# Hybrid attention block on one core: FFN gemms interleaved singly, wide matmuls of a product first, queries ahead of the retention transposes, a table load and a copy moved

## The chip, the core and the metric

The kernel runs on one core of a Trainium2 chip. The core has a matrix engine (TensorE, PE in the profile), a vector engine (VectorE, DVE), an activation engine (ScalarE, ACT), GpSimd (POOL) and SyncE (SP, which here issues most DMA transfers). Each engine takes its own instructions in order and waits on semaphores for the others. Operands lie in SBUF, matmuls write PSUM, which has eight banks of 128 partitions x 512 fp32 numbers. The metric is the device time of one execution in microseconds (us), as the median of several runs.

## The reference

One transformer block for 512 tokens of width 1024, all in fp32. Its core, cut:

```python
mod = einsum('bd,de->be', silu(c), w_ada) + b_ada        # shift1, scale1, gate1, shift2, ...
hmix = modulate(rmsnorm(x, g_norm1), shift1, scale1)
sb_q, sb_k, sb_v, r_q, r_k, r_v, r_g, br = split(einsum('bsd,de->bse', hmix, w_in))
o_sb = stick_breaking_attention(sb_q, sb_k, sb_v)         # 16 heads of 64
o_ret = retention(rotary(r_q), rotary(r_k) * 256 ** -0.5, r_v)   # 4 heads, qk 256, v 512
o_ret = silu(r_g) * head_rmsnorm(o_ret)
g_sb, g_ret = split(sigmoid(br + b_branch))
merged = g_sb * (o_sb @ w_proj_sb) + g_ret * (o_ret @ w_proj_ret)
x = x + gate1 * (merged @ w_out)
hffn = modulate(rmsnorm(x, g_norm2), shift2, scale2)
a, u = split(hffn @ w_ffn_in)                             # 2816 columns each
x = x + gate2 * ((silu(a) * u) @ w_ffn_out)
return rmsnorm(x, g_final)
```

## The kernel before

Everything is kept transposed: features on the partitions, the 512 tokens along the free dimension. The weights come packed in `wp` and stay fp32 in memory. A fp32 product is made of three matmuls in the faster type fp32r: each operand is split into a high and a low part (`split`, L206 on ACT for the high copy, L208 on DVE for the difference), and PE adds high x high, high x low and low x high (`mm3`, all recorded at L228). `gemm` runs this over the pieces `k` of the contraction: a gemm with eight pieces is 24 matmuls, one with four is 12. `weight` loads a raw weight over SP's queue and splits it into `whi` and `wlo`; `low` and `high` (L851, L847) do the same for sums of weights, and `low_dma` has the subtraction done by a DMA.

PSUM's eight banks belong to three pools: `ps` (4), `z` (3) and `av` (1). SBUF tiles come from pools too, with few buffers each (weights: raw 3, whi 4, wlo 4). A scheduler orders the instructions of each engine by when it expects their operands and by their order in the program; in blocks under `manual_schedule` the program's order is kept as written.

**The retention heads.** For each head the queries and keys (`ret_qk`) are two gemms of 24 matmuls each (two halves of 256 features, in two `ps` banks), followed by the rotary multiplications on DVE (from L674 on). The scores and outputs follow (`ret_scores`, `ret_out`), which leave the head's output in four banks (three of `z` and `av`). `ret_gate` finishes a head: four multiplications on DVE, each with the norm's factor and the gate's Silu (L758), then 16 transposes on PE of 128 x 128 blocks into the same pools' banks (L762), whose results are split on ACT and DVE into pairs `s` for the projection. The loop over `h` (L1045 on) does, for heads 0 to 2: the gate of head `h`, the queries and keys of head `h + 1`, and then `seven`, which holds the projection of head `h` (`ret_proj`) and the values and gates of head `h + 1`, computed as seven products of half-size blocks (a scheme of Strassen's kind: sums of blocks of weights and of activations, seven products for eight). Head 3's gate stands ahead of the attention's values (`seven("sv", ...)`), in the mode `first=True`: the first product runs ahead of the gate, and its copies (L991) are on ACT. Just ahead of it `sigmoid_tables` (L329) loads ACT's function table for what follows.

**The FFN.** The 2816 hidden features are 11 blocks `p` of 256. For each `p`, `a` and `u` come from seven products (p, 1) to (p, 7) of the same kind. For p from 2 (`WIDE`) on, a product is `wide_product`: it writes two banks, and for each bank it multiplies the high weight with high and low activations side by side (512 wide) four times, and the low weight with the high activations (256 wide, into the bank's second half) four times. `both_sums` and `both_added` (ACT copy, then DVE additions, L1304 and L1312) empty the two banks. Products 1, 6, 7 and 4 of a `p` share the two `ps` banks called `z`, products 5 and 3 two others, product 2 uses two of the `z` pool. `store_act` splits the result. The second gemm of the FFN (`out`, eight feature blocks, 12 matmuls each) takes the hidden features in chunks of up to two `p`, and its results are added to the residual (L1158).

The list `work` sets the order: the seven products of each `p` as (1, 5, 6, 2, 7, 3, 4), with out gemms of the chunk before in between, two after product 5 and two after product 4. Ahead of each item, the weights of the items up to `AHEAD` places later are loaded and split (`prepare_item`). The FFN's opening (L1480 to L1600) is a manual block: it computes the second norm by halves and runs the products of p = 0, some of p = 1 and the first two of p = 2 in a written order; `held_pe`, `held_act` and `held` are the instructions behind which the scheduler may place what follows.

Of the kernel before, what the change touches and what calls it, by code (L numbers as in the profile page):

```python
# [115 lines left out]
def kernel(  # L116
# [545 lines left out]

    def ret_qk(h, banks=None):
        res = []
        for key in ("rq", "rk"):
            if banks:
                p1, p2 = banks.pop(0), banks.pop(0)
            else:
                p1, p2 = ps(), ps()
                gemm(p1, weight((key, h, 0)), hs)  # L670
                gemm(p2, weight((key, h, 1)), hs)
            for c1, c2, op in ((cosT, sinT, ALU.subtract), (sinT, cosT, ALU.add)):
                m1, m2 = tmp(), tmp()
                nc.vector.tensor_mul(m1, p1, c1)  # L674
                nc.vector.tensor_mul(m2, p2, c2)
                nc.vector.tensor_tensor(m1, m1, m2, op=op)
                hl = pair("q")
                split(hl[:, 0, :], hl[:, 1, :], m1)
                res.append(hl)
        return res  # L680
# [364 lines left out]
    for h in range(3):  # L1045
        ys = ret_gate(h, *outs, sgs)
        qk = ret_qk(h + 1)
        st, outs = {}, []
# [3 lines left out]
        sgs = [rsgs[b] for b in range(4)]  # L1052
    act_table = sigmoid_tables()
    seven("sv", 3, lambda: ret_gate(3, *outs, sgs), sv_store, first=True)

# [186 lines left out]
    def prepare_item(it):  # L1242
        if it[0] == "out":
            ready[it] = out_weight(*it[1:])
            return
# [44 lines left out]
    def wide_product(p, n, banks, first, last):  # L1290
        hi, lo = (tiles(t) for t in ready.pop((p, n)))
        for i, o in enumerate(banks):
            c = slice(i * P, (i + 1) * P)
            for k in range(4):
                mm(o, hi[:, k, c], act7(SEVEN[n], k)[2], first and k == 0, False)
            for k in range(4):
                mm(o[:, 256:S], lo[:, k, c], act7(SEVEN[n], k)[0], False, last and k == 3)
# [109 lines left out]

    def run_out(c, i):
        for j, w in enumerate(ready.pop(("out", c, i))):
            o = psa() if j else psz()  # L1410
            gemm(o, w, ff_acts[c])
            residual(2 * i + j, o, 40)

    NP, NC, AHEAD = NF // 2, len(FF_CHUNKS), 5
    chunk_of = {p: c for c, (p0, n) in enumerate(FF_CHUNKS) for p in range(p0, p0 + n)}
# [4 lines left out]
    for c, (p0, n) in enumerate(FF_CHUNKS):  # L1422
        for p in range(p0, p0 + n):
            wide = p >= 2
            for n_, m in enumerate((1, 6, 5, 2, 7, 3, 4) if p == 1 == WIDE else (1, 5, 6, 2, 7, 3, 4) if wide else (1, 6, 5, 7, 2, 4, 3)):
                if (p, m) not in FIRST:
                    work.append((p, m))
                    if n_ in ((1, 6) if wide else (2, 5)) and len(outs) > (1 if c == NC - 1 else 0):
                        work.append(outs.pop(0))
        work += outs  # L1430
        outs = [("out", c, i) for i in range(4)]
    for m in (2, 1):
# [33 lines left out]
    with tc.manual_schedule(engines={nc.vector.engine, nc.scalar.engine, nc.tensor.engine}):  # L1466
# [114 lines left out]
        nc.vector.tensor_add(d1["s0"], d1["x2"], d1["p1"])  # L1581
        for d in (d0, d1):
            nc.scalar.activation(d["s0"], d["s0"], AF.Silu)
        d0["u3"] = tmp()
# [4 lines left out]
        k6 = high(t1[6], wtile("whi"))  # L1589
        nc.scalar.activation(d0["u3"], d0["u3"], AF.Silu)  # L1590
        d2 = part.setdefault(2, {})
        d2["x"] = ps()
        product(2, 1, d2["x"], True, False)
        d2["p1"] = tmp()
        held_act = nc.scalar.activation(d2["p1"], d2["x"], AF.Copy).ins
        ready[1, 6] = low(t1[6], k6, wtile("wlo"))
# [19 lines left out]
    for it in work:  # L1616
# [3 lines left out]
        with after_opening():  # L1620
            (run_out if it[0] == "out" else run_product)(*it[-2:])
    ln_exp_tables()
# [167 lines left out]
```

## Time and profile before

| | |
|---|---|
| median of 3 runs | 1121.58 us |
| lowest and highest | 1119.62 and 1122.04 us |
| the profiled execution | 1119.72 us |
| its span | 1118.0 us |
| mean granted TensorE clock | 0.997 |
| PE busy | 1101.4 us (99%) |
| DVE busy | 876.9 us (78%) |
| ACT busy | 562.4 us (50%) |
| POOL busy | 42.2 us (4%) |

The profile records one execution. A row of a timeline has the start of a group of like instructions in us from the span's start, the time from the first's start to the last's end, engine, source line, operation, the tiles written and read (buffer numbers left out), the shape, the count, and in brackets the idle time of the engine ahead of the group with the engine and line that ended it. Matmuls are pipelined, so the length in a row is longer than what a matmul adds: the distance from one start to the next tells the pace. The rows use the lines of the kernel before; a weight `whi` or `wlo` belongs to the gemm whose matmuls read it.

### The profile page before, as it was taken

How to read it: one execution, taken by the hardware profiler on the slowest of the kernel's cores; microseconds unless marked ns; L12 is line 12 of the kernel's file. 1: busy time of each engine (PE TensorE's matmuls, PEld its weight loads, DVE VectorE, ACT ScalarE, POOL GpSimd, SP SyncE). 2: the span in 40 equal slices, each digit the busy share in tenths (PEclk: the TensorE clock that was granted, in tenths of full speed). 3: DMA queues.
4: the chain of work that ended last, by engine and by line, in shares of the span. 5: the costliest groups of instructions: out<-in, count | busy, mean ns of one | idle time of the engine just before them, and what ended most of it. 6: DMA issues, size and time to landing. Idle time of an engine off the chain costs nothing.

```text
span 1118.0 us, 15104 instructions
## 1 busy us (share of the span) xinstructions
PE 1101.4 (99%) x5607; PEld 934.7 (84%) x5607; DVE 876.9 (78%) x1315; ACT 562.4 (50%) x926; POOL 42.2 (4%) x69
## 2 busy tenths in 40 slices
PE   8999999999999999999999999999999999999996
PEld 6888888888788788888888888899988888888886
DVE  7899756959977969387777866567999988888866
ACT  5445345444444645365565654357645544554443
POOL 0000000010020020000000000000000000000000
PEclk9999999999999999999999999999999999999998
DMA  9814432766785476876676459662444444444112
GB/s 360 301 57 152 145 118 79 224 133 207 244 168 179 160 163 214 241 208 184 171 200 173 141 182 311 207 170 58 132 133 132 132 132 123 123 132 128 62 38 77
DMA packets 60554, 181.42 MB, mean 162 GB/s; under 512 B 7488, under 2 KB 9536, under 8 KB 60480
## 3 DMA queue, kind: packets, MB, share of 16 engines
q1 hardware_dynamic: 54464, 166.30, 45.9%
q0 software_dynamic: 5472, 13.63, 7.7%
q8 instruction: 44, 0.72, 0.3%
q10 hardware_dynamic: 544, 0.52, 0.1%
q14 instruction: 30, 0.25, 0.1%
HBM read 148.97 MB, written 16.78 MB: 148 GB/s over the span
## 4 chain that ended last, share of the span: by engine, by line
PE 82%; DVE 11%; DMA 3%; ACT 2%; issue 1%; SPq 0%; DVEq 0%; ACTq 0%
PE ps L228 61%; PE z L228 12%; PE av L228 7%; DMA araw<-wada 3%; DVE araw L256 2%; DVE wlo L851 1%; PE ps L636 1%; DVE s L870 1%; DVE wlo L208 1%; DMA sraw<-wada 1%; DVE t L758 0%; ACT whi L847 0%; PE z L762 0%; DVE s L209 0%; DVE t L1033 0%
## 5 line engine op out<-in xcount | busy, mean ns | idle before, releaser
L228 PE MATMUL ps<-h,whi 128*128 128x512 f32 (+1 forms) x1026 | 294.9, 372 | 0.0
L228 PEld LDWEIGHTS ps<-h,whi 128*128 128x128 f32 x1026 | 185.3, 189 | 32.0 <-issue 0.5
L206 ACT ACTIVATE whi<-raw 128x1024 fp32r<-128x1024 f32 (+1 forms) x104 | 108.6, 1044 | 195.7 <-PE ps L228 154.8
L228 PE MATMUL ps<-h,wlo 128*128 128x512 f32 (+1 forms) x513 | 188.0, 370 | 0.0
L208 DVE TENSOR_TENSOR wlo<-raw,whi 128x1024 fp32r<-128x1024 f32 (+1 forms) x104 | 125.0, 1201 | 65.1 <-ACT whi L206 64.6
L228 PEld LDWEIGHTS ps<-h,wlo 128*128 128x128 f32 x513 | 96.7, 188 | 16.7
L228 PE MATMUL ps<-q,whi 128*128 128x512 f32 (+1 forms) x368 | 103.8, 388 | 0.0
L228 PE MATMUL ps<-s,whi 128*128 128x512 f32 x320 | 98.9, 390 | 0.5 <-DVE s L208 0.3
L851 DVE TENSOR_TENSOR wlo<-s,whi 128x1024 fp32r<-128x1024 f32 x46 | 56.1, 1222 | 42.3 <-ACT whi L847 42.3
L228 PEld LDWEIGHTS ps<-q,whi 128*128 128x128 f32 x368 | 65.2, 188 | 10.9
L847 ACT ACTIVATE whi<-s 128x1024 fp32r<-128x1024 f32 x47 | 49.6, 1057 | 45.6 <-PE ps L228 35.0
L228 PE MATMUL ps<-whi,h 128*128 128x512 f32 x222 | 71.7, 391 | 0.0
L228 PEld LDWEIGHTS ps<-s,whi 128*128 128x128 f32 x320 | 60.1, 188 | 13.5 <-DVE s L208 0.6
L228 PE MATMUL ps<-q,wlo 128*128 128x256 f32 (+1 forms) x328 | 63.4, 291 | 0.0
L228 PE MATMUL ps<-s,wlo 128*128 128x512 f32 x160 | 62.2, 389 | 0.0
L228 PEld LDWEIGHTS ps<-q,wlo 128*128 128x128 f32 x328 | 51.7, 189 | 5.7
L228 PEld LDWEIGHTS ps<-whi,h 128*128 128x128 f32 x222 | 41.7, 188 | 9.6 <-ACT t L991 1.1
L1303 ACT ACTIVATE t<-ps 128x256 f32<-128x256 f32 x82 | 30.7, 374 | 32.8 <-PE ps L228 32.7
L256 DVE SCALAR_TENSOR_TENSOR araw<-araw,cact 128x1024 f32<-128x1024 f32 x32 | 39.1, 1229 | 7.2 <-DMA araw<-wada 7.2
L228 PE MATMUL ps<-wlo,h 128*128 128x512 f32 x111 | 43.2, 390 | 0.0
L228 PE MATMUL ps<-whi,q 128*128 128x512 f32 x128 | 40.7, 389 | 0.0
L847 ACT ACTIVATE whi<-h 128x1024 fp32r<-128x1024 f32 x20 | 21.2, 1060 | 37.9 <-PE av L228 29.1
(346 smaller groups left out, 2221.6 us busy)
## 6 DMA issues: line engine op xcount, KB each, us to landing
raw<-wp SPq DMA_DIRECT2D x136, 512.0 KB, 4.0
araw<-wada SPq DMA_DIRECT2D x32, 512.0 KB, 4.0
araw<-wp SPq DMA_DIRECT2D x30, 512.0 KB, 4.5
s<-wp SPq DMA_DIRECT2D x24, 512.0 KB, 5.9
sraw<-wada SPq DMA_DIRECT2D x16, 512.0 KB, 8.7
q<-qp SPq DMA_DIRECT2D x32, 256.0 KB, 4.5
spill<-o POOLq DMA_DIRECT2D x24, 256.0 KB, 5.1
s<-wp POOLq DMA_DIRECT2D x9, 512.0 KB, 6.9
```

The lines of the kernel that those rows point to most:

```text
L206: nc.scalar.activation(dst_hi, src, AF.Copy, scale=scale)
L208: return (eng or nc.vector).tensor_sub(dst_lo, src, f(dst_hi))
L228: return nc.tensor.matmul(o, lhs, rhs, start=start, stop=stop, skip_group_check=True).ins
L256: nc.vector.scalar_tensor_tensor(raw, raw, 1.0, cact, op0=ALU.mult, op1=ALU.mult, accum_out=col)
L636: nc.tensor.transpose(at[bank][:, c : c + P], t[:, a + j * P : a + (j + 1) * P], ident)
L847: nc.scalar.activation(hi, t, AF.Copy)
L851: nc.vector.tensor_sub(lo, t, f(hi))
L870: nc.vector.tensor_tensor(dst[:, d], *((y, x) if swap else (x, y)), op=op)
L1303: nc.scalar.activation(c, o[:, 0:256], AF.Copy)
```

## The change

It has five parts.

1. `ret_qk` has a new argument `between`, called between the two gemms of the queries. The head loop passes the gate of the head before through it, so that the queries' first gemm stands ahead of the gate in the program and the transposes between the two gemms.
2. `sigmoid_tables` moves from ahead of `seven("sv", ...)` to behind head 3's gate.
3. In the opening, the copy of product (2, 1) out of its bank moves on ACT from behind the three Silus to behind the first, and the name `held_act` goes to the last Silu.
4. `wide_product` runs the 512-wide matmuls of both banks first and then the 256-wide ones of both.
5. The out gemms are items of their own (`run_out(c, i, j)`), placed singly after products 5, 2, 3 and 4 of a wide `p`. A pair's weights are prepared with its first gemm. `AHEAD` goes from 5 to 4.

```diff
--- before.py
+++ after.py
@@ -660,7 +660,7 @@
 
     head_pe = {}
 
-    def ret_qk(h, banks=None):
+    def ret_qk(h, banks=None, between=lambda: None):
         res = []
         for key in ("rq", "rk"):
             if banks:
@@ -668,6 +668,8 @@
             else:
                 p1, p2 = ps(), ps()
                 gemm(p1, weight((key, h, 0)), hs)
+                if key == "rq":
+                    between()
                 gemm(p2, weight((key, h, 1)), hs)
             for c1, c2, op in ((cosT, sinT, ALU.subtract), (sinT, cosT, ALU.add)):
                 m1, m2 = tmp(), tmp()
@@ -1043,15 +1045,22 @@
         pass
     outs = ret_out(0, st, vt)
     for h in range(3):
-        ys = ret_gate(h, *outs, sgs)
-        qk = ret_qk(h + 1)
+        ys = []
+        qk = ret_qk(h + 1, between=lambda: ys.extend(ret_gate(h, *outs, sgs)))
         st, outs = {}, []
         vt = lambda: [rvts[b] for b in range(4)]
         seven(("vg", h + 1), h, lambda: ys, rv_store, lambda: st.update(ret_scores(h + 1, qk)),
               lambda: outs.extend(ret_out(h + 1, st, vt())))
         sgs = [rsgs[b] for b in range(4)]
-    act_table = sigmoid_tables()
-    seven("sv", 3, lambda: ret_gate(3, *outs, sgs), sv_store, first=True)
+    table_load = []
+
+    def last_gate():
+        ys = ret_gate(3, *outs, sgs)
+        table_load.append(sigmoid_tables())
+        return ys
+
+    seven("sv", 3, last_gate, sv_store, first=True)
+    act_table = table_load[0]
 
     diag = table(consts[:, NCON + 2 * S :])
     stick_sets = sticks()
@@ -1241,7 +1250,9 @@
 
     def prepare_item(it):
         if it[0] == "out":
-            ready[it] = out_weight(*it[1:])
+            _, c, i, j = it
+            if j == 0:
+                ready["out", c, i] = out_weight(c, i)
             return
         p, n = it
         if p > 1 and n == (5 if p >= WIDE else 6):
@@ -1293,6 +1304,8 @@
             c = slice(i * P, (i + 1) * P)
             for k in range(4):
                 mm(o, hi[:, k, c], act7(SEVEN[n], k)[2], first and k == 0, False)
+        for i, o in enumerate(banks):
+            c = slice(i * P, (i + 1) * P)
             for k in range(4):
                 mm(o[:, 256:S], lo[:, k, c], act7(SEVEN[n], k)[0], False, last and k == 3)
 
@@ -1405,15 +1418,14 @@
             for j in range(2)
         ]
 
-    def run_out(c, i):
-        for j, w in enumerate(ready.pop(("out", c, i))):
-            o = psa() if j else psz()
-            gemm(o, w, ff_acts[c])
-            residual(2 * i + j, o, 40)
-
-
-
-    NP, NC, AHEAD = NF // 2, len(FF_CHUNKS), 5
+    def run_out(c, i, j):
+        o = psa() if j else psz()
+        gemm(o, ready["out", c, i].pop(0), ff_acts[c])
+        residual(2 * i + j, o, 40)
+
+
+
+    NP, NC, AHEAD = NF // 2, len(FF_CHUNKS), 4
     chunk_of = {p: c for c, (p0, n) in enumerate(FF_CHUNKS) for p in range(p0, p0 + n)}
     ff_acts = {c: [] for c in range(NC)}
     FIRST = [(0, 1), (0, 2), (1, 1), (0, 4), (1, 2), (0, 6), (0, 5), (0, 7)]
@@ -1421,14 +1433,17 @@
     outs = []
     for c, (p0, n) in enumerate(FF_CHUNKS):
         for p in range(p0, p0 + n):
-            wide = p >= 2
-            for n_, m in enumerate((1, 6, 5, 2, 7, 3, 4) if p == 1 == WIDE else (1, 5, 6, 2, 7, 3, 4) if wide else (1, 6, 5, 7, 2, 4, 3)):
+            wide = p >= WIDE
+            kept = 2 if c == NC - 1 else 0
+            for m in (1, 5, 6, 2, 7, 3, 4) if wide else (1, 6, 5, 7, 2, 4, 3):
                 if (p, m) not in FIRST:
                     work.append((p, m))
-                    if n_ in ((1, 6) if wide else (2, 5)) and len(outs) > (1 if c == NC - 1 else 0):
+                    count = (m in (5, 2, 3, 4,)) if wide else 2 * (m in (5, 4))
+                    while count and len(outs) > kept:
                         work.append(outs.pop(0))
+                        count -= 1
         work += outs
-        outs = [("out", c, i) for i in range(4)]
+        outs = [("out", c, i, j) for i in range(4) for j in range(2)]
     for m in (2, 1):
         work.remove((2, m))
     work[:1] = [(2, 1), (0, 3), (2, 2)]
@@ -1579,20 +1594,20 @@
         nc.scalar.activation(d0["c22"], d0["v"], AF.Copy)
         d1["s0"] = tmp()
         nc.vector.tensor_add(d1["s0"], d1["x2"], d1["p1"])
-        for d in (d0, d1):
-            nc.scalar.activation(d["s0"], d["s0"], AF.Silu)
+        nc.scalar.activation(d0["s0"], d0["s0"], AF.Silu)
+        d2 = part.setdefault(2, {})
+        d2["x"] = ps()
+        product(2, 1, d2["x"], True, False)
+        d2["p1"] = tmp()
+        nc.scalar.activation(d2["p1"], d2["x"], AF.Copy)
+        nc.scalar.activation(d1["s0"], d1["s0"], AF.Silu)
         d0["u3"] = tmp()
         nc.vector.tensor_add(d0["u3"], d0["w"], d0["u2"])
         nc.vector.tensor_add(d0["c22"], d0["c22"], d0["u3"])
         nc.vector.tensor_add(d0["u3"], d0["y"], d0["u3"])
         t1 = sums_of[1]
         k6 = high(t1[6], wtile("whi"))
-        nc.scalar.activation(d0["u3"], d0["u3"], AF.Silu)
-        d2 = part.setdefault(2, {})
-        d2["x"] = ps()
-        product(2, 1, d2["x"], True, False)
-        d2["p1"] = tmp()
-        held_act = nc.scalar.activation(d2["p1"], d2["x"], AF.Copy).ins
+        held_act = nc.scalar.activation(d0["u3"], d0["u3"], AF.Silu).ins
         ready[1, 6] = low(t1[6], k6, wtile("wlo"))
         sums(1, t7="h")
         product(0, 3, d0["v"], False, True, late="w")
@@ -1618,7 +1633,10 @@
             with after_opening():
                 prepare_item(queue.pop(0))
         with after_opening():
-            (run_out if it[0] == "out" else run_product)(*it[-2:])
+            if it[0] == "out":
+                run_out(*it[1:])
+            else:
+                run_product(*it)
     ln_exp_tables()
```

How the instructions stand on the engines shows the effect. First PE at head 2's queries (head 2 of 0 to 3; the tiles `h_...` are the activations, `ps_2511` the bank of the queries' first gemm, `t_1853`, `t_1854`, `t_2347` and `t_2348` the four gated outputs, `z` and `av` the transposes' banks). Before:

```order
L228 MATMUL ps_2511<-h_391,whi_2515 128x512 x2
L228 MATMUL ps_2511<-h_391,wlo_2516 128x512
L762 MATMUL z_2455<-con,t_1853 128x128
L762 MATMUL z_2456<-con,t_1853 128x128
L762 MATMUL av_2458<-con,t_1853 128x128
L228 MATMUL ps_2511<-h_438,whi_2515 128x512 x2
L762 MATMUL z_2455<-con,t_1854 128x128
L762 MATMUL z_2455<-con,t_2347 128x128
L762 MATMUL z_2455<-con,t_2348 128x128
L762 MATMUL z_2456<-con,t_1854 128x128
L762 MATMUL z_2456<-con,t_2347 128x128
L762 MATMUL z_2456<-con,t_2348 128x128
```

After (`ps_2451` is now the bank of the first gemm):

```order
L228 MATMUL ps_2451<-h_486,whi_2455 128x512 x2
L228 MATMUL ps_2451<-h_486,wlo_2456 128x512
L228 MATMUL ps_2451<-h_525,whi_2455 128x512 x2
L228 MATMUL ps_2451<-h_525,wlo_2456 128x512
L764 MATMUL z_2487<-con,t_1853 128x128
L764 MATMUL z_2487<-con,t_1854 128x128
L764 MATMUL z_2487<-con,t_2347 128x128
L764 MATMUL z_2487<-con,t_2348 128x128
L764 MATMUL z_2488<-con,t_1853 128x128
L764 MATMUL z_2488<-con,t_1854 128x128
```

The transposes stood within the gemm, after its fifteenth matmul, two of its matmuls among them; now the gemm is complete ahead of the first transpose, and the sixteen follow in a block.

Next PE at a wide product of the FFN (two banks each, `ps_8262` and `ps_8263` before, `ps_8256` and `ps_8257` after):

```order
L228 MATMUL ps_8262<-v_6764,s_8098 128x512 x2
L228 MATMUL ps_8262<-v_6765,s_8098 128x512 x2
L228 MATMUL ps_8262<-v_6764,s_8099 128x256 x2
L228 MATMUL ps_8262<-v_6765,s_8099 128x256 x2
L228 MATMUL ps_8263<-v_6764,s_8098 128x512 x2
L228 MATMUL ps_8263<-v_6765,s_8098 128x512 x2
L228 MATMUL ps_8263<-v_6764,s_8099 128x256 x2
L228 MATMUL ps_8263<-v_6765,s_8099 128x256 x2
```

```order
L228 MATMUL ps_8256<-q_7082,whi_8304 128x512 x2
L228 MATMUL ps_8256<-q_7083,whi_8304 128x512 x2
L228 MATMUL ps_8257<-q_7082,whi_8304 128x512 x2
L228 MATMUL ps_8257<-q_7083,whi_8304 128x512 x2
L228 MATMUL ps_8256<-q_7082,wlo_8306 128x256 x2
L228 MATMUL ps_8256<-q_7083,wlo_8306 128x256 x2
L228 MATMUL ps_8257<-q_7082,wlo_8306 128x256 x2
L228 MATMUL ps_8257<-q_7083,wlo_8306 128x256 x2
```

Two groups of 512 wide and two of 256 wide alternated; now all wide ones come first, and both banks are complete only at the end.

Last ACT in the FFN's opening (`t_6954` and `t_7167` are the Silus' tiles of p = 0 and p = 1, `t_7203` and `t_7195` the copy of product (2, 1), `whi` a weight's high part). Before:

```order
L1583 ACT_TABLE_LOAD
L1583 ACTIVATE t_6954<-t_6954 128x512
L1583 ACTIVATE t_7167<-t_7167 128x512
L847 ACTIVATE whi_7175<-s_7163 128x1024
L1590 ACTIVATE t_7171<-t_7171 128x512
L1595 ACTIVATE t_7203<-ps_7178 128x512
```

After:

```order
L1597 ACT_TABLE_LOAD
L1597 ACTIVATE t_6954<-t_6954 128x512
L1602 ACTIVATE t_7195<-ps_7170 128x512
L1603 ACTIVATE t_7167<-t_7167 128x512
L849 ACTIVATE whi_7202<-s_7163 128x1024
L1610 ACTIVATE t_7198<-t_7198 128x512
```

The copy, from the `ps` bank, moved from the end of this stretch to behind the first Silu.

## The prediction

> **What bounds the kernel now.** I read the page's head first, then its chain of work that ended last, then the timeline of TensorE (PE) at each place that the diff touches, with the engine that released it, and last the busy time by stage. The page's span, its busy line and the first line of its chain:
>
> ```profile
> span 1118.0 us, 15104 instructions
> PE 1101.4 (99%) x5607; PEld 934.7 (84%) x5607; DVE 876.9 (78%) x1315; ACT 562.4 (50%) x926; POOL 42.2 (4%) x69
> PE 82%; DVE 11%; DMA 3%; ACT 2%; issue 1%; SPq 0%; DVEq 0%; ACTq 0%
> ```
>
> PE is busy for 1101.4 of 1118.0 us, so 16.6 us are idle in all. The change takes no matmul away and adds none, so it can win only from idle stretches and from matmuls that follow each other more slowly than they could. Each place is therefore priced by PE's cadence there. In the FFN a second engine is near its limit, as the busy time by stage shows (columns: length, then PE, PE's weight loads, DVE, ACT, POOL, clock, DMA):
>
> ```profile
> 820.00:840.00 20.00, 20.00 (x109) 17.19 (x108) 20.00 (x34) 8.60 (x11) 0.00 (x0) 1.00 0.49 130
> 840.00:860.00 20.00, 20.00 (x109) 17.18 (x108) 19.30 (x32) 10.61 (x16) 0.87 (x1) 1.00 0.51 143
> ```
>
> VectorE (DVE) has no room from 820 to 840. What PE gains just ahead of that stretch it may have to give back there.
>
> **Queries ahead of the transposes.** Head 2's gate, then the same for heads 1 and 0 (timelines of PE and DVE; columns: start, length of the group, engine, line, operation, tiles, count, idle before with its releaser):
>
> ```profile
> 282.72 0.61 PE L228 MATMUL ps<-h,whi 128*128 128x512 f32 x2
> 285.89 0.39 PE L228 MATMUL ps<-h,wlo 128*128 128x512 f32 x1
> 287.29 0.44 PE L762 MATMUL z<-con,t 128*128 128x128 f32 x2 [1.01 <-DVE t L758]
> 288.14 1.25 PE L762 MATMUL z<-con,t 128*128 128x128 f32 x10
> 289.23 0.49 PE L762 MATMUL av<-con,t 128*128 128x128 f32 x3
> 291.18 0.61 PE L228 MATMUL ps<-h,whi 128*128 128x512 f32 x2
> 286.49 1.41 DVE L758 SCALAR_TENSOR_TENSOR t<-z,sm,t 128x512 f32<-128x512 f32 x2
> ```
>
> ```profile
> 188.24 0.61 PE L228 MATMUL ps<-h,whi 128*128 128x512 f32 x2
> 195.84 0.62 PE L228 MATMUL ps<-h,whi 128*128 128x512 f32 x2
> 191.16 1.41 DVE L758 SCALAR_TENSOR_TENSOR t<-z,sm,t 128x512 f32<-128x512 f32 x2
> ```
>
> ```profile
> 93.44 0.62 PE L228 MATMUL ps<-h,whi 128*128 128x512 f32 x2
> 101.21 0.70 PE L228 MATMUL ps<-h,whi 128*128 128x512 f32 x2
> 97.52 2.07 DVE L758 SCALAR_TENSOR_TENSOR t<-z,sm,t 128x512 f32<-128x512 f32 x3
> 99.50 0.74 DVE L758 SCALAR_TENSOR_TENSOR t<-av,sm,t 128x512 f32<-128x512 f32 x1
> ```
>
> In head 2 fourteen 512-wide matmuls stand between 282.72 and 285.89: 3.17 / 14 = 0.2264, so with what the other rows give I use 0.2267 us. Ten transposes take 289.23 − 288.14 = 1.09, so 0.109 each. From the first matmul of the queries' first gemm to that of their second, 24 matmuls and 16 transposes are due: 24 × 0.2267 + 16 × 0.109 = 7.18.
>
> - Head 2 takes 291.18 − 282.72 = 8.46 and loses 1.28, because a transpose stands in PE's queue before its operand is there. Afterwards the whole gemm runs first and ends at 282.72 + 5.44 = 288.16, when the last multiply of the gate has ended (286.49 + 1.41 = 287.90). Nothing is left to wait for. I take −1.24 and keep 0.04 for the change of width.
> - Head 1 takes 7.60 and loses 0.42. The gate ends at 192.57, the gemm would end at 193.68: −0.38.
> - Head 0 takes 7.77 and loses 0.59, but its gate ends at 100.24 and the gemm already at 98.88. The third operand comes at 97.52 + 2.07 = 99.59, the fourth at 100.24. Eight transposes are still to do by then (the new order puts the fourth operand's into the last eight places): 100.30 + 8 × 0.109 = 101.17, against 101.21. The wait is now for DVE instead of being filled by gemm: −0.03.
>
> What this delays: the splits of the transposed operands on ACT and DVE, 1 to 2 us later, behind a weight split and a rotary multiply. Their users are the projections behind three more gemms (3 × 5.44 = 16 us), so they cost nothing. On SP's queue the raw weight of the next key gemm now goes ahead of loads that the splits free; it moves by the same 1 to 2 us under the same 16 us. Bounds of the three together: 0 (each wait is replaced) to −2.3 (all of 1.28 + 0.42 + 0.59).
>
> **The table load.** Head 3's end on ACT, DVE and PE:
>
> ```profile
> 382.00 1.28 ACT L329 ACT_TABLE_LOAD   x1
> 385.21 1.57 ACT L206 ACTIVATE s<-z 128x512 fp32r<-128x512 f32 x3
> 387.11 1.10 ACT L206 ACTIVATE whi<-raw 128x1024 fp32r<-128x1024 f32 x1
> 383.68 1.22 DVE L969 TENSOR_TENSOR s<-araw,s 128x1024 f32<-128x1024 f32 x1
> 385.94 1.89 DVE L208 TENSOR_TENSOR s<-z,s 128x512 fp32r<-128x512 f32 x3
> 388.34 1.22 DVE L208 TENSOR_TENSOR wlo<-raw,whi 128x1024 fp32r<-128x1024 f32 x1
> 385.86 0.49 PE L228 MATMUL ps<-s,whi 128*128 128x512 f32 x1 [0.18 <-ACT s L206]
> 386.69 0.49 PE L228 MATMUL ps<-s,whi 128*128 128x512 f32 x1 [0.34 <-DVE s L208]
> ```
>
> PE waits twice, 0.18 for ACT and 0.34 for DVE, and with the slow start of each matmul behind a wait that is about 0.9 us. The load moves from 382.00 to behind the four splits, so ACT can split up to 1.28 earlier. DVE cannot: between 383.68 and 385.94 it does two operations of 1.13 whatever their order, and PE's second wait is for DVE at 385.94. So the first wait goes and the second grows: 0. Bounds: −0.9 if both go, +0.3 if DVE's new order is the worse one. The weight at 387.11 then comes 1.28 later at most; its low half ends at 388.34 + 1.28 + 1.22 = 390.8. PE uses it behind two gemms of 12 that began at 385.86, not before 385.86 + 24 × 0.2267 = 391.3: hidden, with 0.5 to spare.
>
> The Trainium skill, "ScalarE: Activation LUTs", section "What ACT_TABLE_LOAD costs", puts a switch at about 2.66 us, the load and a drain of 1.38. By it the low half would end at 392.2 and PE would wait 0.9, so the sum would be 0.9 worse. The row does not bear the drain out: here the load takes 1.28 and ACT's next group, at 383.29, starts as it ends.
>
> **The FFN's opening.**
>
> ```profile
> 793.27 2.08 PE L228 MATMUL z<-q,whi 128*128 128x256 f32 x16
> 795.19 1.12 PE L228 MATMUL z<-q,wlo 128*128 128x256 f32 x8
> 797.47 3.14 PE L228 MATMUL ps<-v,h 128*128 128x256 f32 x24 [1.16 <-ACT t L1595]
> 803.32 0.40 PE L228 MATMUL z<-qp,whi 128*128 128x256 f32 x2
> 794.18 0.63 ACT L1583 ACTIVATE t<-t 128x512 f32<-128x512 f32 x1 [2.94 <-DVE t L1581]
> 796.83 0.58 ACT L1595 ACTIVATE t<-ps 128x512 f32<-128x512 f32 x1
> 801.39 1.22 DVE L851 TENSOR_TENSOR wlo<-s,whi 128x1024 fp32r<-128x1024 f32 x1
> ```
>
> Sixteen 256-wide matmuls take 795.19 − 793.27 = 1.92, 0.12 each. Product (0,3) is over at 795.19 + 8 × 0.12 = 796.15. Product (2,2) adds into the bank that the copy of L1595 reads, and starts at 797.47: 1.32 lost. The copy's input is complete when PE goes to (0,3), at 793.27, but ACT takes its queue in order and sits idle for 2.94 before the Silu at 794.18. With the copy ahead of that Silu it runs in ACT's idle time, from about 793.5 to 794.1, and (2,2) starts at 796.15. The Silu still starts when DVE lets it.
>
> What is late next: DVE's weight split, 801.39 to 802.61, which the next product's third matmul needs. That product started at 803.32; 1.32 earlier, its third matmul is due at 802.00 + 0.24 = 802.24 and waits 0.37, with a slow start some 0.45. Net −0.87. Bounds: −1.32 (DVE also gets ahead) to 0 (DVE sets the pace until the end of its full stretch).
>
> **Wide matmuls first, out gemms singly.** A wide product writes two banks, with four 512-wide and four 256-wide matmuls each. Before, the width changes after every four (512, 256, 512, 256), now after every eight.
>
> ```profile
> 806.20 0.63 PE L228 MATMUL z<-s,whi 128*128 128x512 f32 x2
> 808.95 0.40 PE L228 MATMUL z<-q,whi 128*128 128x256 f32 x2
> 900.93 1.30 PE L228 MATMUL ps<-v,s 128*128 128x512 f32 x6
> 931.50 0.84 PE L228 MATMUL ps<-v,s 128*128 128x512 f32 x3
> ```
>
> From 900.93 to 931.50 PE does one p: seven products and four out gemms of 12, that is 7 × 8 + 4 × 12 = 104 wide and 56 narrow matmuls. It takes 30.57; the cadences give 104 × 0.22667 + 56 × 0.12 = 30.29. The 0.28 that is left, over 14 changes to narrow and back, is 0.02 each. A run of 12 wide ones between narrow ones (806.20 to 808.95) takes 2.75 against 2.72, so 0.03 for one change. Nine p have wide products, less the two in the opening: 61 products, one change fewer in each. At 0.02 that is −1.2. If the changes that stay cost 0.03, a p keeps 0.21 of its 0.28 and over 61 / 7 = 8.7 p only 0.6 is won. Between the two I take −0.9; bounds 0 and −2.4 (all of 0.28 × 8.7).
>
> Against it stands a rule: the Trainium skill, "TensorE: Matmul & The Clock Gate", section "Back-to-back issue gap", gives an isolated matmul N/2.4 + 2.5 ns by its own width alone, without a price for a change. By it this term is 0 and the sum −2.5. The rows differ already in the cadence (227 and 120 ns, where the rule has 216 and 109), and a remainder of 0.28 is there.
>
> The out gemms, two at a time before, are spread singly, with the same matmuls. The items are finer and four instead of five are prepared ahead, so a weight split comes later but still before its use by several microseconds; no weight waits in the rows of a p (30.57 leaves only 0.28). 0. What shrinks is the time in which a product's banks must be emptied, and that is the rival on the other side.
>
> **Sum.** −1.24 − 0.38 − 0.03 + 0 − 0.87 − 0.9 = −3.4 us. The profiled execution took 1119.72 (its span and 1.72 around it), which would become 1116.3. The median of the runs is 1121.58, two of the three being near 1122; against it the forecast is 1118.2. Less than 0.2% (2.2 us) either way is about what a measurement of this kernel can't tell from no change.
>
> **The rivals.**
>
> - *Banks emptied late (slower).* Product (p+1,1) writes the two banks of (p,4). Before, two out gemms lie between (5.44 us), now one (2.72). And with the wide matmuls first, the first bank is complete only 4 × 0.12 = 0.48 before the product's end, where it was 1.39. So that bank must be empty within 3.2 us, the second within 2.72 + 4 × 0.2267 = 3.6. How long emptying takes, from a product whose successor on PE starts at 914.78:
>
> ```profile
> 914.78 2.97 PE L228 MATMUL z<-v,h 128*128 128x512 f32 x16
> 916.75 0.41 DVE L1304 TENSOR_TENSOR t<-t,ps 128x256 f32<-128x256 f32 x1
> ```
>
>   The second bank is read until 917.16, 2.4 us after the product, so 1.2 is to spare. One more weight split of 1.22 ahead of the addition uses that up, two make PE wait 1.2 us at each of the eight borders between two p: +9.8 − 3.4 = +6.4, 1128. It decides from 0.43 us a border. For it speaks a DVE that is full from 820 to 840; against it, the 1.2 to spare.
> - *Changes of width are free* (as the rule above has it): −2.5, 1119.1.
> - *DVE takes the opening's gain back.* The queue that is full until 840 fixes PE's progress: −3.4 + 0.87, 1119.0.
> - *Only the gates' waits go*, the FFN as a whole unmoved: −1.65, 1119.9, no change that can be told.
>
> **How the numbers follow.** The whole sum 0.50; free changes of width 0.14; opening given back 0.10; gates only 0.05; banks late 0.17; and 0.04 for more gain than the sum, up to the bounds above. The two at 1119 lie at the edge of 0.2% (1119.3), so about half of each counts as the same; of the whole sum 0.03 does. Faster 0.47 + 0.08 + 0.06 + 0.04 = 0.65, same 0.03 + 0.06 + 0.04 + 0.05 = 0.18, slower 0.17. The range reaches from 1115.4, the sum against the profiled execution less about 1, to 1122.0: the cases without late banks hold 0.8, and the bottom of that case adds little. The likeliest case's own range is 1116 to 1119.3.
>
> **What would show it.** Right: at head 2's gate PE goes from one gemm to the transposes without an idle stretch, 7.2 us from first to second gemm, and at head 1's as well, while head 0 shows a wait of some 0.7 for L760's multiply; PE goes from (0,3) to (2,2) without a wait, and then waits some 0.4 for DVE's weight split near 802; a p takes 30.4 instead of 30.57. Wrong: waits of TensorE on the addition that empties a bank, at the first matmul of (p+1,1), eight times; or a wait for weights in the FFN, since fewer are prepared ahead; or a wait near 391 for the weight behind the table load.

## The result

| | before | changed |
|---|---|---|
| median of six runs | 1120.68 us | 1117.03 us |
| lowest and highest | 1119.62 to 1122.04 | 1115.6 to 1118.46 |
| profiled execution, its span | 1119.72, 1118.0 | 1117.28, 1115.6 |

The ratio is 0.9965 with a 95% interval of 0.9952 to 0.9978; the medians differ by 3.7 us. Forecast were 1118.2 and a gain of 3.4. The forecast time was counted from a median of three runs, 1121.58; from the median of six the same gain gives 1117.3.

The two profiled spans differ by 2.4 only, and the places show why. First the gates of heads 2 and 0 in the changed kernel (timeline of PE):

```profile
283.78 0.61 PE L228 MATMUL ps<-h,whi 128*128 128x512 f32 x2
289.23 1.59 PE L764 MATMUL z<-con,t 128*128 128x128 f32 x12
291.01 0.70 PE L228 MATMUL ps<-h,whi 128*128 128x512 f32 x2
```

```profile
93.61 0.62 PE L228 MATMUL ps<-h,whi 128*128 128x512 f32 x2
99.06 0.44 PE L764 MATMUL z<-con,t 128*128 128x128 f32 x2
99.83 1.32 PE L764 MATMUL z<-con,t 128*128 128x128 f32 x10 [0.33 <-DVE t L760]
101.34 0.71 PE L228 MATMUL ps<-h,whi 128*128 128x512 f32 x2
```

At head 2 the wait of 1.01 is gone; from gemm to gemm it takes 7.23 where it took 8.46. Head 0 takes 7.73 (7.77 before) and waits inside the transposes instead of ahead of them; the idle time shown is 0.33, where the prediction named some 0.7. Head 1 takes 195.44 − 188.33 = 7.11 (7.60 before):

```profile
188.33 0.62 PE L228 MATMUL ps<-h,whi 128*128 128x512 f32 x2
195.44 0.71 PE L228 MATMUL ps<-h,whi 128*128 128x512 f32 x2
```

The FFN's opening, PE, then ACT and DVE:

```profile
792.81 2.08 PE L228 MATMUL z<-q,whi 128*128 128x256 f32 x16
794.73 1.12 PE L228 MATMUL z<-q,wlo 128*128 128x256 f32 x8
795.68 3.04 PE L228 MATMUL ps<-v,h 128*128 128x256 f32 x24
802.11 0.50 PE L228 MATMUL z<-s,whi 128*128 128x512 f32 x1 [0.26 <-ACT s L206]
793.01 0.60 ACT L1602 ACTIVATE t<-ps 128x512 f32<-128x512 f32 x1 [2.25 <-PE ps L228]
800.90 1.22 DVE L853 TENSOR_TENSOR wlo<-s,whi 128x1024 fp32r<-128x1024 f32 x1
```

The copy runs at 793.01 and product (2,2) follows (0,3) without a gap: 794.73 + 8 × 0.12 = 795.69. The new wait near 802 is there; counted from start to start, 0.42 is lost. One p of the FFN, and the new wait that nothing had foretold:

```profile
899.30 1.52 PE L228 MATMUL ps<-v,s 128*128 128x512 f32 x6
929.73 2.93 PE L228 MATMUL ps<-v,s 128*128 128x512 f32 x16
```

```profile
268.87 0.51 PE L228 MATMUL ps<-wlo,q 128*128 128x512 f32 x1 [0.86 <-DVE wlo L853]
264.43 1.23 DVE L256 SCALAR_TENSOR_TENSOR araw<-araw,cact 128x1024 f32<-128x1024 f32 x1 [2.63 <-DMA araw<-wada]
267.61 1.21 DVE L853 TENSOR_TENSOR wlo<-s,whi 128x1024 fp32r<-128x1024 f32 x1
```

A p takes 30.43 instead of 30.57. At 268.87 PE waits for a weight's low half; DVE makes it at 267.61, behind a multiplication for the modulation (L256) that itself waited 2.63 us for its transfer. Counted from start to start this wait costs 1.13, and it was not in the profile of before.

Summed by place. What a stretch takes beyond the cadences of its matmuls (0.2267 us for a 512-wide one, 0.12 for a 256-wide one, 0.109 for a transpose) counts as lost; the third column gives the changed kernel's profile less that of before:

| place | forecast | two profiles |
|---|---|---|
| gates of heads 0, 1, 2 | −0.03, −0.38, −1.24 | −0.04, −0.49, −1.23 |
| head 3 | 0 | −0.13 (0.95 lost before, 0.82 after) |
| opening | −0.87 | −1.32 + 0.42 = −0.90 |
| FFN from 840 to 1080 | −0.9 | −1.0 (2.14 lost before, 1.13 after) |
| 268 | not named | +1.13 |

That makes −2.7 for the spans' −2.4. Without the wait at 268 it is −3.8, near the 3.7 of the medians. This nearness is partly chance: a second profile of the changed kernel, from another comparison, has a span of 1112.9 and loses 0.23 at head 3 where the first lost 0.82.

### The profile page after: what moved, and what is told of

Read it like the earlier page. It is cut to its first block, busy times and chain, and to the rows that moved or that the text cites. A ratio compares the mean times of both kernels' runs of the same rounds, so it can differ in the third digit from the quotient of the medians.

```text
span 1115.6 us, 15072 instructions
## 1 busy us (share of the span) xinstructions
PE 1100.7 (99%) x5607; PEld 936.9 (84%) x5607; DVE 876.6 (79%) x1315; ACT 561.5 (50%) x926; POOL 42.2 (4%) x69
## 4 chain that ended last, share of the span: by engine, by line
PE 87%; DVE 8%; DMA 2%; ACT 2%; issue 1%; DVEq 0%; ACTq 0%
PE ps L228 64%; PE z L228 13%; PE av L228 8%; DMA araw<-wada 2%; PE ps L636 1%; DVE s L872 1%; DVE wlo L853 1%; DVE araw L256 1%; DVE wlo L208 0%; PE z L764 0%; DVE t L760 0%; DVE s L209 0%; ACT whi L849 0%; PE av L636 0%; ACT q L1187 0%
## 5 line engine op out<-in xcount | busy, mean ns | idle before, releaser
L228 PE MATMUL ps<-q,whi 128*128 128x512 f32 (+1 forms) x368 | 98.5, 386 | 0.0
L228 PEld LDWEIGHTS ps<-q,whi 128*128 128x128 f32 x368 | 68.0, 188 | 13.4 <-DVE t L1325 0.2
L228 PE MATMUL ps<-q,wlo 128*128 128x256 f32 (+1 forms) x328 | 59.4, 293 | 0.0
L228 PEld LDWEIGHTS ps<-q,wlo 128*128 128x128 f32 x328 | 48.2, 190 | 3.3
L256 DVE SCALAR_TENSOR_TENSOR araw<-araw,cact 128x1024 f32<-128x1024 f32 x32 | 39.1, 1229 | 9.6 <-DMA araw<-wada 9.4
L228 PE MATMUL z<-q,q 128*128 128x256 f32 (+3 forms) x224 | 40.0, 324 | 0.0
L626 DVE TENSOR_TENSOR_SCAN s<-s,table 128x1024 f32<-128x1024 f32 x16 | 36.6, 2290 | 2.1 <-ACT s L620 2.1
```

The source lines that it names most:

```text
L228: return nc.tensor.matmul(o, lhs, rhs, start=start, stop=stop, skip_group_check=True).ins
L256: nc.vector.scalar_tensor_tensor(raw, raw, 1.0, cact, op0=ALU.mult, op1=ALU.mult, accum_out=col)
L626: nc.vector.tensor_tensor_scan(n[:, ::-1], n[:, ::-1], d[:, ::-1], 0.0, op0=ALU.mult, op1=ALU.max)
```

## The experiments

Each comparison is with the kernel before, run on the same chip; its median was 1119.6 to 1120.4.

**The queries alone.** Part 1 of the change and nothing else:

```diff
                 gemm(p1, weight((key, h, 0)), hs)
+                if key == "rq":
+                    between()
                 gemm(p2, weight((key, h, 1)), hs)
...
-        ys = ret_gate(h, *outs, sgs)
-        qk = ret_qk(h + 1)
+        ys = []
+        qk = ret_qk(h + 1, between=lambda: ys.extend(ret_gate(h, *outs, sgs)))
```

> Kernel before with part 1 alone (the queries' first gemm ahead of the gate's transposes). By my sum the three gates give 0.03 + 0.38 + 1.24 = 1.65 us: 1120.68 - 1.65 = 1119.0, with no idle stretch of TensorE at the gates of heads 1 and 2 and 0.3 to 0.6 at head 0. In the profile of the changed kernel a new wait of 1.13 us stands at 267.5, for a weight's low half that DVE makes behind a multiplication that waits for a modulation weight's DMA. Theory A: part 1 causes it by the later transfers on SP's queue; then it stands here too, at about 267, and the time is 1120.1. Theory B: it is the DMA's spread from one execution to the next; then it is as likely in a kernel without part 1.

Measured 1117.73, ratio 0.9986 (0.9977 to 0.9995): 1.6 us faster by the ratio, with an interval of 0.6 to 2.6 around the 1.65 of the sum. There is no wait at 267 in its profile, which speaks against theory A.

**The wide matmuls alone.** Part 4:

```diff
                 mm(o, hi[:, k, c], act7(SEVEN[n], k)[2], first and k == 0, False)
+        for i, o in enumerate(banks):
+            c = slice(i * P, (i + 1) * P)
             for k in range(4):
                 mm(o[:, 256:S], lo[:, k, c], act7(SEVEN[n], k)[0], False, last and k == 3)
```

> Kernel before with part 4 alone (both banks' 512-wide matmuls first). My theory: a change of width costs about 0.02 us, so TensorE's loss in a p of the FFN halves, from 0.28 to 0.14, and the whole is 0.6 to 1.2 us faster: 1119.5 to 1120.1. Rival (changes of width are free, the FFN's gain in the changed kernel comes from the single out gemms): the loss in a p stays 0.28, 1120.7.

Measured 1122.47, ratio 1.0028 (1.0018 to 1.0038): 3 us slower, which neither theory had. The waits of TensorE in its FFN (engine and tile, who was waited for, us in all, times, longest), and one of the places:

```profile
PE ps L228 <- DVE t L1306: 3.0, 3, 1.6
```

```profile
946.01 2.95 PE L228 MATMUL z<-v,h 128*128 128x512 f32 x16
950.17 2.12 PE L228 MATMUL ps<-q,whi 128*128 128x512 f32 x8 [1.21 <-DVE t L1306]
946.77 1.22 DVE L851 TENSOR_TENSOR wlo<-h,whi 128x1024 fp32r<-128x1024 f32 x1
947.91 0.74 DVE L1158 SCALAR_TENSOR_TENSOR o<-av,mod,o 128x512 f32<-128x512 f32 x1
948.57 1.21 DVE L208 TENSOR_TENSOR wlo<-raw,whi 128x1024 fp32r<-128x1024 f32 x1
949.70 0.74 DVE L1306 TENSOR_TENSOR t<-t,ps 128x256 f32<-128x256 f32 x2
```

Product 6 is over at 946.01, product 2 runs into other banks, and product 7 is to write product 6's banks again. Only 2.77 us lie between, so it is due at 948.8 and starts at 950.17. DVE makes the low halves of two weights and a residual first, and its additions out of the banks (L1306) run from 949.70. Before, the first bank of product 6 was complete 1.39 us ahead of the product's end and product 7 came to its second bank 1.39 after its start; with the wide ones first these are 0.48 and 0.91. That is less time for the same work of DVE. The undisturbed p keep 0.18 lost in 40 us (880 to 920) where before has 0.35, so the gain from the order is there too and is outweighed.

**Widths alternating one by one**, on the changed kernel:

```diff
             for k in range(4):
                 mm(o, hi[:, k, c], act7(SEVEN[n], k)[2], first and k == 0, False)
-        for i, o in enumerate(banks):
-            c = slice(i * P, (i + 1) * P)
-            for k in range(4):
                 mm(o[:, 256:S], lo[:, k, c], act7(SEVEN[n], k)[0], False, last and k == 3)
```

> Changed kernel, but each bank's 512-wide and 256-wide matmuls alternate one by one: eight changes to narrow and back in a product where the changed kernel has one. My theory (0.02 us a change): 7 x 7 more changes in a p, 49 x 0.02 = 0.98 us, over 8.7 p 8.5 us: 1117.0 + 8.5 = 1125.5. If a change costs 0.03, 1129.8. Rival (free): 1117.0.

Measured 1119.87, ratio 1.0001 (0.9992 to 1.0010). That is 2.8 us above the changed kernel's median, and 4.0 by the two ratios to the kernel before, each taken on its own chip; the forecast was 8.5. Its p:

```profile
898.90 2.97 PE L228 MATMUL ps<-v,s 128*128 128x512 f32 x16
929.65 2.51 PE L228 MATMUL ps<-v,s 128*128 128x512 f32 x13
```

30.75 against 30.43: 0.32 for 49 more changes is 0.0065 each, over 8.7 p 2.8 us, a third of the forecast. So the order of widths has a price, but it isn't 0.02 for each change. The starts of the matmuls, between 850 and 1085, show why. In the changed kernel's runs of eight and more, the first five wide matmuls behind narrow ones are slow and take 27.3 ns too long together, and the narrow run gives 7.6 back: 0.020 for a change. A wide matmul that stands alone between narrow ones pays once, 9.6 ns, and the narrow one gives 3.3 back: 0.006.

**No out gemm between two p**, on the changed kernel:

```diff
-                    count = (m in (5, 2, 3, 4,)) if wide else 2 * (m in (5, 4))
+                    count = (m in (5, 2, 3)) + (m == 3) if wide else 2 * (m in (5, 4))
```

> Changed kernel, but no out gemm between product (p,4) and product (p+1,1); it goes to product 3 of the same p, so the same matmuls run. This takes the 2.72 us away in which the two banks are emptied. By the rows of before a bank is read until 2.4 us after its product; TensorE needs the second bank 0.91 us after it starts, so it should wait 1.5 us at each of the eight borders: +12 us, 1129 (bounds 0.8 to 2.4 us a border, 1123 to 1136). If TensorE doesn't wait there, emptying was never near the limit and my slower rival had no ground: 1117.0.

Measured 1116.98, ratio 0.9977 (0.9965 to 0.9989), which is not apart from the changed kernel, and no wait of TensorE for a bank in its FFN. The prediction's slower rival had the wrong banks. One border, PE with products (p,4) and (p+1,1), then DVE's additions out of the banks of (p,4):

```profile
927.12 1.98 PE L228 MATMUL ps<-q,whi 128*128 128x512 f32 x8
928.94 1.11 PE L228 MATMUL ps<-q,wlo 128*128 128x256 f32 x8
929.89 2.96 PE L228 MATMUL ps<-v,s 128*128 128x512 f32 x16
930.65 0.74 DVE L1317 TENSOR_TENSOR t<-t,ps 128x256 f32<-128x256 f32 x2
```

Product (p+1,1) starts at 929.89 without a gap and is in its second bank from 930.80, while DVE still reads the banks of (p,4) until 931.39. So it writes other banks. That they are those of (p,3), free a whole product earlier, would fit, but no trace names the banks.

**The wide matmuls with the single out gemms.** Parts 4 and 5 on the kernel before; the second adds to the diff of part 4:

```diff
-    def run_out(c, i):
+    def run_out(c, i, j):
...
-    NP, NC, AHEAD = NF // 2, len(FF_CHUNKS), 5
+    NP, NC, AHEAD = NF // 2, len(FF_CHUNKS), 4
...
+                    count = (m in (5, 2, 3, 4,)) if wide else 2 * (m in (5, 4))
+                    while count and len(outs) > kept:
                         work.append(outs.pop(0))
+                        count -= 1
```

> Kernel before with parts 4 and 5 (wide matmuls first, out gemms singly). Part 4 alone made the kernel 3 us slower: TensorE waited three times (1.2, 1.6, 0.2 us) at product 7's first matmul for DVE's additions that empty the banks of product 6, since only product 2 lay between. Theory A: the single out gemms cover this, as one of them now stands between products 2 and 7; then these waits are gone, the loss of TensorE in a p is 0.14 instead of 0.27 and the kernel 1.0 us faster than before: 1118.6 against 1119.6. Theory B: the waits come from what DVE has to do for prepared weights, whose order part 5 changes too little; then a part of them stays, 1120 or more.

Measured 1119.31, ratio 0.9993 (0.9982 to 1.0004). By the time alone this is no change, though it is 0.0035 below part 4 alone, with intervals apart. The trace has no wait for a bank, and TensorE loses 0.18 in 40 us from 880 on, and 1.15 from 840 to 1080 where before loses 2.14: the 1.0 of theory A. So part 5 takes away the waits that part 4 brings.

**The single out gemms alone:**

```diff
-    NP, NC, AHEAD = NF // 2, len(FF_CHUNKS), 5
+    NP, NC, AHEAD = NF // 2, len(FF_CHUNKS), 4
...
-            wide = p >= 2
+            wide = p >= WIDE
+            kept = 2 if c == NC - 1 else 0
```

> Kernel before with part 5 alone (out gemms singly, four items ahead). Before, nothing waits for a bank in the FFN, so theory A has nothing to win here: 1119.6, the loss in a p 0.27 as before. If single gemms were worth something by themselves (fewer changes of width, better cover), it would be below 1119.

Measured 1120.26, ratio 1.0003 (0.9993 to 1.0013): no change. TensorE loses 0.42 in 40 us from 880 on, a little more than before (0.35), and 2.76 from 840 to 1080 (2.14 before).

**The gap ahead of product 7**, on the changed kernel: two out gemms behind product 5, none behind product 2.

```diff
-                    count = (m in (5, 2, 3, 4,)) if wide else 2 * (m in (5, 4))
+                    count = 2 * (m == 5) + (m in (3, 4)) if wide else 2 * (m in (5, 4))
```

> Changed kernel with the out gemm that stood between products 2 and 7 moved up behind product 5, beside the one there; the rest stays single. With wide matmuls first, product 7 then writes the first bank of product 6 again 0.48 + 2.77 = 3.2 us after it is complete, as in the kernel with part 4 alone. My theory: that gap is what cost part 4 alone its 3 us; so waits for DVE's addition stand at some of the eight products 7, 0.2 to 1.8 us each, together 1 to 5 us, and the time is 0.9975 to 1.001 of before where the changed kernel has 0.9964. Rival: part 4 alone was slow for what DVE had to do in another place (five items prepared ahead, two out gemms after product 4); then no wait stands at product 7 here and the time is that of the changed kernel.

Measured 1117.94, ratio 0.9975 (0.9964 to 0.9987), at the lower end of the expectation and not apart from the changed kernel. Its profile against the changed kernel's at the same p, first the changed kernel:

```profile
910.37 2.96 PE L228 MATMUL z<-v,h 128*128 128x512 f32 x16
915.91 1.98 PE L228 MATMUL ps<-q,whi 128*128 128x512 f32 x8
913.62 0.74 DVE L1317 TENSOR_TENSOR t<-t,ps 128x256 f32<-128x256 f32 x2
```

```profile
912.37 2.95 PE L228 MATMUL z<-v,h 128*128 128x512 f32 x16
915.73 2.11 PE L228 MATMUL ps<-q,whi 128*128 128x512 f32 x8 [0.41 <-DVE t L1317]
915.26 0.75 DVE L1317 TENSOR_TENSOR t<-t,ps 128x256 f32<-128x256 f32 x2
```

In the changed kernel the additions end at 914.36, 4.0 us after product 6, and product 7 comes 5.5 after it: 1.5 to spare, thanks to the out gemm between. Without that gemm product 7 is due 2.8 us after product 6, at 915.2, and waits 0.41 for the first of the two additions, which ends near 915.7. This is one wait in eight p, where part 4 alone has three and longer ones. So the gap is a condition of the waits but doesn't set their size; what else does (five items prepared ahead instead of four, two out gemms behind product 4) was not told apart.

**The copy alone.** Part 3:

```diff
-        for d in (d0, d1):
-            nc.scalar.activation(d["s0"], d["s0"], AF.Silu)
+        nc.scalar.activation(d0["s0"], d0["s0"], AF.Silu)
+        d2 = part.setdefault(2, {})
+        d2["x"] = ps()
+        product(2, 1, d2["x"], True, False)
+        d2["p1"] = tmp()
+        nc.scalar.activation(d2["p1"], d2["x"], AF.Copy)
+        nc.scalar.activation(d1["s0"], d1["s0"], AF.Silu)
```

> Kernel before with part 3 alone (the copy of product (2,1) ahead of two Silus on ACT). My theory: the 1.3 lost ahead of product (2,2) go, and about 0.45 come back near 802, where DVE's queue has no gap: -0.87, 1118.7. Rival: DVE's full stretch from 820 to 840 takes back the rest, then TensorE's loss between 800 and 860 grows by 0.87 more and the time is that of before.

Measured 1119.24, ratio 0.9994 (0.9984 to 1.0005); 0.7 us, inside the interval. The trace tells it better: no loss ahead of (2,2) any more, 0.44 at 803.9, and between 840 and 1080 the same losses as before. The rest is not given back.

**The table load alone.** Part 2:

```diff
-    act_table = sigmoid_tables()
-    seven("sv", 3, lambda: ret_gate(3, *outs, sgs), sv_store, first=True)
+    def last_gate():
+        ys = ret_gate(3, *outs, sgs)
+        table_load.append(sigmoid_tables())
+        return ys
+
+    seven("sv", 3, last_gate, sv_store, first=True)
```

> Kernel before with part 2 alone (the table load behind head 3's splits). My theory: the first of TensorE's two waits at 386 (0.35 lost) goes, and the second, for DVE (0.60 lost), takes it up: 0, 1120.0. In the changed kernel the two came to 0.82 together instead of 0.95. Rival: moving the load is worth the 0.4 that the profile of the changed kernel shows between 360 and 400; then the stretch loses 0.9 where it lost 1.3.

Measured 1119.96, ratio 0.9996 (0.9985 to 1.0006). TensorE has one wait there that loses 0.95, where before two lost 0.35 and 0.60: the forecast 0. The stretch from 360 to 400 loses 1.02 instead of 1.31; the difference lies in small waits among the transposes ahead of it, 0.17 of it at 383.54 in the profile of before.

**Two more edits on the changed kernel**, and the changed kernel beside them:

```diff
-                if key == "rq":
+                if key == "rq" and h > 1:
                     between()
                 gemm(p2, weight((key, h, 1)), hs)
+                if key == "rq" and h == 1:
+                    between()
...
-            elif i == 3:
+            elif i == 3 and first:
+                with tc.issue_after(last_split[0].ins):
+                    sub(b12, b11, b11)
+            elif i == 3:
                 sub(b12, b11, b11)
```

> Changed kernel with two more edits: head 0's gate goes behind the second gemm of head 1's queries instead of the first, and head 3's subtraction of weights on DVE is held back until the gate's splits. At head 0 TensorE then finds all four operands ready (they come at 100.3, the second gemm ends at 104.3): -0.55. At head 3 the low splits can begin when ACT's high parts are there, 384.8 instead of 385.4, so of the 0.82 that is lost at least 0.5 goes. Together -1.0, against the changed kernel 1116.0 (0.9957 of before). If the delayed operands or the held subtraction are needed sooner than I think, new waits stand at 110 to 120 and near 392.

> The changed kernel once more, for two things. The wait of 1.13 us near 267 for a low half behind DVE's modulation row: in seven other profiles it was 0 in five, 0.3 in one, 0.5 in two, with and without part 1 among them. By theory B (the DMA's spread) it should be another number here, most likely under 0.6; by theory A (caused by part 1) it is about 1.1 again. And the time beside that of the next kernel on the same chip: 0.9965 of before.

> The kernel with head 0's gate one gemm later and head 3's subtraction held, on the same chip as the changed kernel. Its profile lost 0.55 less at head 0 and 0.6 less at head 3; if nothing else moved, it is 1.1 us faster than the changed kernel, 0.9955 of before, which five rounds can just tell or not.

The two edits measured 1115.79, ratio 0.9964 (0.9949 to 0.9978), and again 1115.45, ratio 0.9962 (0.9947 to 0.9976). The changed kernel, in the same comparison as the second of these, measured 1115.63, ratio 0.9963 (0.9949 to 0.9977). The times don't separate them. In the profile head 0's wait is gone (0.54 lost in the changed kernel, none with the edits). Head 3 loses 0.23 with the edits, but also in the second profile of the changed kernel, which lost 0.82 there in its first. So nothing shows that holding the subtraction wins anything, and half of the expected 1.0 is missing. The spans were 1112.9 for the changed kernel and 1112.5 with the two edits.

The changed kernel's second profile has no wait near 268. On DVE the two rows read:

```profile
262.94 1.23 DVE L256 SCALAR_TENSOR_TENSOR araw<-araw,cact 128x1024 f32<-128x1024 f32 x1 [1.23 <-DMA araw<-wada]
266.11 1.22 DVE L853 TENSOR_TENSOR wlo<-s,whi 128x1024 fp32r<-128x1024 f32 x1
```

The transfer was there 1.5 us earlier, and the low half with it. Over all fourteen profiles, TensorE is idle there in five: 0.86 and 0.36 in two of the eight with part 1, and 0.33, 0.13 and 0.07 in three of the six without it (the copy alone, the wide matmuls alone, the table load alone). So part 1 isn't needed for it, and the same program has it or not; this fits theory B, though it doesn't exclude that part 1 makes the wait longer.

## Why the prediction was right, and where it was wrong

The time (1117.0 for 1118.2), the sign and the terms of the sum held. Of the 1.2 us by which the time is off, 0.9 is the median that it was counted from, and 0.3 the gain.

- *The gates* came out as worked out, head by head, and part 1 alone gave 1.6 for its 1.65. Head 1 won 0.49 instead of 0.38: 16 transposes in one block took 195.44 − 193.78 = 1.66, 0.104 each instead of 0.109, and the 0.04 kept for the change of width was not needed.

```profile
193.78 1.47 PE L764 MATMUL z<-con,t 128*128 128x128 f32 x12
```

- *The opening* won 1.32 and gave 0.42 back, where 0.45 had been set down for DVE's weight split. The wait that the trace names is another one: the scheduler put a first out matmul there, which waits for ACT's split that it reads. The limit that the prediction named stands all the same: DVE's weight split ends at 800.90 + 1.22 = 802.12, so the third matmul, due at 801.69, would have waited about as long without the out matmul.
- *The table load* was worth nothing that can be told, and what it delays stayed hidden. Of a drain behind it, as the Trainium skill, "ScalarE: Activation LUTs", section "What ACT_TABLE_LOAD costs", has it, the changed kernel's trace shows none either; ACT's next weight follows at once:

```profile
386.29 1.28 ACT L329 ACT_TABLE_LOAD   x1
387.58 1.06 ACT L206 ACTIVATE whi<-raw 128x1024 fp32r<-128x1024 f32 x1
```

- *The wide matmuls first* won 1.0 from 840 to 1080, which is 7.9 of the 8.7 p, for the 0.9 forecast. The rival that has changes of width free, as a formula by width alone in the Trainium skill, "TensorE: Matmul & The Clock Gate", section "Back-to-back issue gap", would have it, fell: the same matmuls take 30.57, 30.43 or 30.75 for one p by their order alone. But the step "0.02 each" was wrong as a price of every change. It is right for the runs of eight that the change leaves, and right on average for the runs before, where a run of four costs 0.015 and a run of 28 (two out gemms and four matmuls of a product) 0.04; alternating ones cost a third of it.
- *Part 5 at 0* was right as a difference in its own time (1.0003) and wrong as a reading of what it does. The prediction weighed part 4's shorter time for emptying banks at the border between two p only. The place where it is short is between products 6 and 7. Without part 5, part 4 makes the kernel 3 us slower there. That the sum held in spite of this is luck: the change happens to hold the part that takes these waits away. The working had the mechanism, with additions on DVE behind weight splits, and its price, 1.2 us and more, but looked for it in the wrong place. It called the drain 2.4 us from one row, while part 4 alone showed 4.4 (946.01 to 950.44).
- *The step on the banks' rotation* ("Product (p+1,1) writes the two banks of (p,4)") was false in the kernel without an out gemm at the border, where DVE still read those banks 1.5 us after the start of (p+1,1). For the other kernels no trace shows it, but none of them waits there.
- *The transfers on SP's queue* were said to move by 1 to 2 us. The first of head 2's parts `s`, issued at 191.65 before, is issued at 196.47 now, 4.8 later; no wait follows from it.

```profile
191.65 0.90 SPq L915 DMA_DIRECT2D s<-wp  x2
```

```profile
196.47 0.42 SPq L917 DMA_DIRECT2D s<-wp  x1
```

## What to carry to other kernels

Price a reordering on the bound engine by its start-to-start times at the place, and carry it to the next wait in the queue: the terms here came out within some 0.15 us that way, in one pair of profiles. Where one edit shortens the time in which a bank is emptied, list every pair of products that share a bank, with what lies between, from the order that was built and not from the pool's sizes. Parts of a change that look worth nothing alone may be what makes another part pay, so test them together and apart.

## What the runs showed of the hardware

- What a change between wide and narrow matmuls costs depends on the lengths of the runs. In the changed kernel (850 to 1085, 52 whole runs of wide behind narrow ones) the first five wide matmuls of a run take 233.4, 236.1, 228.4, 232.0 and 231.1 ns on average, where later ones take 226.6, and the first narrow one 113.7 instead of 120. Alternating one by one, a wide and a narrow one take 236.3 and 116.7, 6.3 above the cadence together. Why the surcharge falls on the wide ones behind narrow ones was not tested.
- DVE's order is fixed, so one late transfer of a modulation row holds up all that stands behind it. Between two executions of the same program this moved a weight's low half by 1.5 us (266.11 to 267.61) and turned a wait of TensorE on or off.
